# Low parts of the first feed-forward's weight tiles: by an accumulating DMA instead of VectorE

## The chip, the cores and the metric

The kernel runs on one core of a Trainium2 chip. The metric is the device time of one launch in microseconds, less being better. The engines are named as in the profile: PE (TensorE), DVE (VectorE), ACT (ScalarE), POOL (GpSimd), SP (SyncE, which here only issues DMAs).

## The reference

One inference step of a streaming encoder with two layers, on 1024 prompt frames and 64 sample frames of 1024 channels (1088 columns in all). Layer 0 mixes by windowed attention, layer 1 by a state-space model (SSM); each layer ends with a gated feed-forward with a causal convolution of width 3:

```python
def layer(x, i):
    h = rms_norm(x, g_pre)
    y = attention(h) if i == 0 else s5(h)
    x = x + rms_norm(y, g_post)
    h = rms_norm(x, g_pre_ffn)
    u = causal_conv(h @ w_up[i]) + b          # 1024 -> 2 * 2816
    y = (gelu(u[:2816]) * u[2816:]) @ w_down[i]
    return x + rms_norm(y, g_post_ffn)
```

All of it is float32, and so are the inputs and outputs. The part that matters here is `h @ w_up[0]`.

## The kernel before

**Split products.** PE multiplies in a rounded 32-bit form (fp32r). To keep float32's accuracy each operand is split into a high part, the value rounded to that form, and a low part, the rest. A product is then three matmuls in a row (`mm3`, L223 to L225): high weight by low activation, high by high, low weight by high activation.

**Weight tiles.** A weight tile is 128 x 1024 float32. `load_unit` loads it into a buffer `raw` (two of them) through SP's queue (L208 for `w_up`), and `split_unit` makes the split tile `whl` (six buffers, tag "big"):

```python
x = nc.scalar.activation(w[:, 0], raw, AF.Copy), nc.vector.tensor_sub(w[:, 1], raw, w[:, 0].bitcast(F32))
```

ACT copies raw to the high part, which rounds it; DVE subtracts that from raw and leaves the low part. Both are on L216, and both halves of `whl` are read by PE. `wsrc` lists the tiles in the order of use; `unit` hands out the next one, after `load_ahead` has asked for two more (AHEAD = 2).

**The first feed-forward.** `w_up[0]` has 44 tiles, taken as pairs 0 and 22, 1 and 23, 2 and 24, and so on: a gate tile and a value tile. For each of them PE makes the up-projection of three blocks of columns (384, 384 and 320; `up_block`, 8 x 3 matmuls each) into one of six PSUM buffers, and DVE scales it into `u` (L414). `conv` runs the convolution on ACT (L422) and DVE (L423, L424), `gate` multiplies the pair and stores it to DRAM as `gd` (L441, L442). The first three tiles (0, 22, 1) run side by side, block by block, since their blocks of activations become ready one after the other.

**The passage from attention to it.** For each block `post_norm` loads the residual `xl` (L317), multiplies by the norm (L328) and adds the residual (L331, on DVE or POOL), and the sum is stored as the new `x` (L1565). `pre_norm` then makes the activations' high part `hh` on ACT (L300) and the low part `hl` on DVE (L306) or, for three of eight slices, on POOL (L303, L304); `rstd` makes the norm (L248 to L291). While this goes on, the loads of the next weight tiles stand in SP's queue between those of `xl` and the stores of `x`.

**Beside the feed-forward.** `sums` prepares operands for the down-projection in a tile `jt`: it loads pieces of `w_down` (L355) or `gd` (L367) through SP, DVE makes four sums and differences (L358 to L361, L370 to L376), and SP stores them as `sd` or `td`. `side` prepares the SSM's tables in eight chunks: DVE and POOL multiply complex numbers (L892 to L897, tiles `m`, `tab`, `w`), PE makes `kps` (L1072) and transposes `w` into `wps` (L1083), DVE makes `kt` (L1076, L1077).

**What sets the order.** A scheduler puts each engine's instructions and each queue's DMAs into one fixed order when the kernel is built, by a simulation with priorities; each engine then runs its list in that order, and a step that waits holds back what stands behind it on the same engine or queue.

Of the kernel before, what the change touches and what calls it, by code (L numbers as in the profile page):

```python
# [8 lines left out]
F32 = mybir.dt.float32  # L9
F32R = mybir.dt.float32r  # L10
I32 = mybir.dt.int32
AF = mybir.ActivationFunctionType
ALU = mybir.AluOpType
AX = mybir.AxisListType

P = 128
D = 1024
# [5 lines left out]
KF = DFF // P  # L23
# [20 lines left out]
class Core:  # L44
# [133 lines left out]
    def load_unit(self, src):  # L178
        nc = self.nc
        raw = self.wts.tile([P, D], F32, name="raw", tag="raw", bufs=2)  # L180
        if src[0] == "w_part":

            _, i, k, s, kc, mh = src
            n = min(2, KH - k)
            if s == "s":
                ap = self.sd[:, k:k + n, kc, mh]
            else:
                k += KH * kc
                ap = self.a["w_down"][i, k:k + n, :, 512 * mh:512 * mh + 512].rearrange("k p m -> p k m")
            raw = raw[:, :512 * n]  # L190
            self.loaded = nc.sync.dma_start(raw.rearrange("p (k m) -> p k m", k=n), ap)
            w = self.big([P, 2, D], "whl")[:, :, :512 * n]
            nc.scalar.activation(w[:, 0], raw, AF.Copy)  # L193
            nc.vector.tensor_sub(w[:, 1], raw, w[:, 0].bitcast(F32))  # L194
            return w
        if src[0] == "w_sum":
            self.loaded = nc.sync.dma_start(raw.rearrange("p (h q) -> p h q", h=2), self.su[src[1], :, :, src[2]].rearrange("h p q -> p h q"))
            return self.split_unit(raw)
        ap = self.a[src[0]]
        if src[0] == "w_down":  # L200

            _, i, k, mh = src
            ap = ap[i, k:k + 2, :, 512 * mh:512 * mh + 512].rearrange("k p m -> p k m")
            self.loaded = nc.sync.dma_start(raw.rearrange("p (k m) -> p k m", k=2), ap)
        else:
            for i in src[1:]:
                ap = ap[i]
            self.loaded = nc.sync.dma_start(raw, ap)  # L208
        return self.split_unit(raw)

    behind = ()

# [1397 lines left out]
```

## Time and profile before

| | |
|---|---|
| median of three runs | 2240.71 us |
| the three runs | 2235.85, 2241.18, 2240.71 us |
| span of the profiled execution | 2241.6 us (the page gives no other time of it) |
| PE, DVE, ACT, POOL busy | 98%, 75%, 45%, 18% of the span |
| last matmuls of attention | until 366.8 us |
| passage, first part of the up-projection, part with tables beside it | 366.8 to 411, 411 to 602, 602 to 911 us |
| split line L216 on DVE, 340 to 900 us | 42 times, median 1.22 us |

A profile is one execution seen from the chip: for each instruction its line, engine, start and duration, and what released it if its engine stood idle before. A row of a group reads: line, engine, operation, output <- inputs, count. In a row of waits the left side is who waited and the right side what came last, followed by the us in all, the number of waits and the longest. In a timeline the first two numbers are start and duration in us. For a DMA the last number is the median time in us from issue to landing.

### The profile page before, as it was taken

Reading aid. Unit: us, or ns where it says so; the run is one execution under the profiler, and the core shown is the slowest. Engines: PE = TensorE matmul, PEld = TensorE weight load, DVE = VectorE, ACT = ScalarE, POOL = GpSimd, SP = SyncE. Lnnn points to the kernel's source line nnn. Section 1 sums busy time; section 2 is a strip of 40 time slices with the busy share of each in tenths; the row PEclk is TensorE's granted clock in tenths of the full one; section 3 lists DMA queues with packets and bytes.
Section 4 is the critical chain, followed back from the end, with each engine's and each line's share of the span. In section 5 each row is a group of like instructions: output and inputs, shape, how many; then the busy total and the mean of one; then the engine's idle time right before and its main releaser. Section 6 shows DMA issues by size and latency. Waiting matters only on the chain.

```text
span 2241.6 us, 36077 instructions
## 1 busy us (share of the span) xinstructions
PE 2188.9 (98%) x13875; PEld 2114.0 (94%) x13875; DVE 1687.4 (75%) x2954; ACT 1019.1 (45%) x1839; POOL 414.7 (18%) x474
## 2 busy tenths in 40 slices
PE   9999999999999999999998899999999999999997
PEld 8987789999999999999996699999999999999997
DVE  8687648989877877666768865587997788786754
ACT  5256747422333333455534742263444444455543
POOL 5322004200042323100200034352011111110000
PEclk9999999999999999999999999999999999999999
DMA  5100015656345565887749998751266667678773
GB/s 197 38 22 29 20 62 158 246 184 211 111 136 183 181 192 184 253 298 232 229 147 340 272 295 297 261 167 65 96 217 223 236 237 276 209 269 310 224 243 99
DMA packets 208124, 428.48 MB, mean 191 GB/s; under 512 B 23312, under 2 KB 114224, under 8 KB 205008
## 3 DMA queue, kind: packets, MB, share of 16 engines
q1 hardware_dynamic: 175648, 326.56, 44.3%
q0 software_dynamic: 23984, 95.12, 11.9%
q10 hardware_dynamic: 8320, 4.49, 0.9%
q8 instruction: 109, 1.79, 0.3%
q14 instruction: 63, 0.52, 0.1%
HBM read 297.75 MB, written 128.37 MB: 190 GB/s over the span
## 4 chain that ended last, share of the span: by engine, by line
PE 47%; DMA 6%; DVE 5%; ACT 1%; issue 1%; SPq 1%; POOL 0%; DVEq 0%; ACTq 0%; POOLq 0%
PE mm L225 12%; PE mm L223 12%; PE mm L224 12%; DMA raw<-in_w_down 3%; PE pb L223 1%; PE pb L225 1%; PE pa L224 1%; PE pb L224 1%; PE pa L225 1%; PE pa L223 1%; DVE whl L216 1%; ACT whl L216 1%; DMA yd<-ys 1%; DMA pm<-prm 1%; DVE y L328 0%
## 5 line engine op out<-in xcount | busy, mean ns | idle before, releaser
L223 PE MATMUL mm<-hl,whl 128*128 128x384 f32 (+1 forms) x1960 | 643.4, 329 | 3.8 <-DVE hl L306 3.1
L225 PE MATMUL mm<-hh,whl 128*128 128x384 f32 (+1 forms) x1960 | 641.1, 328 | 2.2 <-DVE whl L216 2.2
L224 PE MATMUL mm<-hh,whl 128*128 128x384 f32 (+1 forms) x1960 | 642.3, 328 | 0.0
L223 PEld LDWEIGHTS mm<-hl,whl 128*128 128x128 f32 x1960 | 368.5, 188 | 6.0 <-DVE hl L306 4.5
L225 PEld LDWEIGHTS mm<-hh,whl 128*128 128x128 f32 x1960 | 368.5, 188 | 2.9 <-DVE whl L216 2.9
L224 PEld LDWEIGHTS mm<-hh,whl 128*128 128x128 f32 x1960 | 368.7, 188 | 0.0
L216 ACT ACTIVATE whl<-raw 128x1024 fp32r<-128x1024 f32 x202 | 212.9, 1058 | 333.4 <-PE mm L225 192.2
L216 DVE TENSOR_TENSOR whl<-raw,whl 128x1024 fp32r<-128x1024 f32 x202 | 254.9, 1264 | 111.2 <-ACT whl L216 110.7
L223 PE MATMUL mm<-gt,whl 128*128 128x384 f32 (+1 forms) x968 | 316.8, 327 | 2.6 <-ACT whl L216 1.7
L225 PE MATMUL mm<-gt,whl 128*128 128x384 f32 (+1 forms) x968 | 315.8, 327 | 0.7 <-DVE whl L216 0.7
L224 PE MATMUL mm<-gt,whl 128*128 128x384 f32 (+1 forms) x968 | 315.9, 327 | 0.0
L223 PEld LDWEIGHTS mm<-gt,whl 128*128 128x128 f32 x968 | 181.7, 188 | 3.2 <-ACT whl L216 1.9
L225 PEld LDWEIGHTS mm<-gt,whl 128*128 128x128 f32 x968 | 181.6, 188 | 1.2 <-DVE whl L216 1.2
L224 PEld LDWEIGHTS mm<-gt,whl 128*128 128x128 f32 x968 | 181.7, 188 | 0.0
L194 DVE TENSOR_TENSOR whl<-raw,whl 128x1024 fp32r<-128x1024 f32 x84 | 96.3, 1153 | 69.2 <-ACT whl L193 68.2
L193 ACT ACTIVATE whl<-raw 128x1024 fp32r<-128x1024 f32 x84 | 82.6, 987 | 115.0 <-DMA raw<-sd 50.2
L423 DVE SCALAR_TENSOR_TENSOR t<-u,ppt,t 128x1090 f32<-128x1090 f32 x88 | 123.6, 1407 | 7.9 <-ACT t L422 7.3
L422 ACT ACTIVATE t<-u,ppt 128x1090 f32<-128x1090 f32 x88 | 114.2, 1298 | 24.4 <-DVE u L521 9.2
L424 DVE SCALAR_TENSOR_TENSOR t<-u,ppt,t 128x1090 f32<-128x1090 f32 x88 | 123.3, 1403 | 0.4
L414 DVE TENSOR_TENSOR u<-rb,mm 128x384 f32<-128x384 f32 (+1 forms) x164 | 80.2, 502 | 20.4 <-PE mm L225 15.7
L566 DVE TENSOR_TENSOR gt<-gr,gt 128x768 fp32r<-128x768 f32 (+2 forms) x106 | 89.9, 879 | 7.1 <-ACT gt L565 6.8
L565 ACT ACTIVATE gt<-gr 128x768 fp32r<-128x768 f32 (+2 forms) x106 | 78.4, 773 | 35.6 <-DMA gr<-gd 24.6
(390 smaller groups left out, 4113.4 us busy)
## 6 DMA issues: line engine op xcount, KB each, us to landing
raw<-in_w_up SPq DMA_DIRECT2D x88, 512.0 KB, 4.2
raw<-in_w_down SPq DMA_DIRECT2D x74, 512.0 KB, 4.4
raw<-sd SPq DMA_DIRECT2D x40, 512.0 KB, 4.6
sj<-in_w_up POOLq DMA_DIRECT2D x68, 256.0 KB, 6.1
su<-sj POOLq DMA_DIRECT2D x34, 512.0 KB, 5.8
raw<-su SPq DMA_DIRECT2D x34, 512.0 KB, 4.7
pm<-prm SPq DMA_DIRECT2D x32, 522.0 KB, 8.6
gr<-td SPq DMA_DIRECT2D x40, 384.0 KB, 5.7
```

Source lines behind the costliest of these rows:

```text
L193: nc.scalar.activation(w[:, 0], raw, AF.Copy)
L194: nc.vector.tensor_sub(w[:, 1], raw, w[:, 0].bitcast(F32))
L216: x = nc.scalar.activation(w[:, 0], raw, AF.Copy), nc.vector.tensor_sub(w[:, 1], raw, w[:, 0].bitcast(F32))
L223: nc.tensor.matmul(out, w[:, 0, sl], xl, start=start, stop=False)
L224: nc.tensor.matmul(out, w[:, 0, sl], xh, start=False, stop=False)
L225: self.last_mm = nc.tensor.matmul(out, w[:, 1, sl], xh, start=False, stop=stop)
L414: nc.vector.tensor_mul(u[:, t0 + 2:t0 + 2 + np_], rb[:, t0:t0 + np_], ps[:, :np_])
L422: nc.scalar.activation(t, u[:, 0:T + 2], AF.Identity, bias=cb(m), scale=cw(0, m))
L423: nc.vector.scalar_tensor_tensor(t, u[:, 1:T + 3], cw(1, m), t, op0=ALU.mult, op1=ALU.add)
L424: self.last_conv = nc.vector.scalar_tensor_tensor(t, u[:, 2:T + 4], cw(2, m), t, op0=ALU.mult, op1=ALU.add)
L565: nc.scalar.activation(x[:, 0, u], raw, AF.Copy)
L566: nc.vector.tensor_sub(x[:, 1, u], raw, x[:, 0, u].bitcast(F32))
```

## The change

For the tiles of `w_up[0]` other than 0, 22 and 1, that is 41 of 44, the split is made in another way. ACT copies raw to the high part as before, and copies raw a second time, with scale -1, to the low part's place, which rounds to the negated high part. A DMA from POOL's queue then adds raw onto it, which leaves raw minus the high part. DVE has no step in it. `raw` is free when that DMA has landed. All later lines move by 11 numbers.

```diff
             self.loaded = nc.sync.dma_start(raw, ap)
+        if src[0] == "w_up" and src[1] == 0 and src[2] not in (0, KF, 1):
+            return self.split_by_dma(raw)
         return self.split_unit(raw)
+
+    def split_by_dma(self, raw):
+
+        nc = self.nc
+        w = self.big([P, 2, D], "whl")
+        nc.scalar.activation(w[:, 0], raw, AF.Copy)
+        nc.scalar.activation(w[:, 1], raw, AF.Copy, scale=-1.0)
+        nc.gpsimd.dma_start(w[:, 1].bitcast(F32), raw, accum_op=ALU.add)
+        return w
```

PE's instructions are the same in number and kind, and SP's DMAs are the same; DVE has 41 steps less, ACT 41 more, POOL issues 41 DMAs more. The scheduler also lays the lists out anew. Three places follow.

SP's queue in the passage, before: the loads of weight tiles 24, 3 and 25 come after that of tile 2, all ahead of block 1's `xl`, with the store of `x` (block 0) and the first `jt` behind.

```order
L208 DMA raw_4657<-in_w_up 128x1024
L909 DMA tq_4269<-in_s_c 128x32x32
L208 DMA raw_4765<-in_w_up 128x1024
L208 DMA raw_4885<-in_w_up 128x1024
L317 DMA xl_3634<-in_x 128x2x384
L317 DMA xl_3635<-in_x 128x2x384
L317 DMA xl_3839<-in_x 128x2x320
L1565 DMA x0_90<-q_410 1024x1x384
L317 DMA xl_3840<-in_x 128x2x320
L355 DMA jt_4581<-in_w_down 128x2x1024
```

The same after (L208 is still the load; 11 is added to the other line numbers; tile 24 is raw_4659, tile 3 raw_4768, tile 25 raw_4889). Each of the three loads now waits for the accumulating DMA of the tile two before it.

```order
L208 DMA raw_4659<-in_w_up 128x1024
L208 DMA raw_4768<-in_w_up 128x1024
L328 DMA xl_3634<-in_x 128x2x384
L328 DMA xl_3635<-in_x 128x2x384
L208 DMA raw_4889<-in_w_up 128x1024
L328 DMA xl_3839<-in_x 128x2x320
L1576 DMA x0_90<-q_410 1024x1x384
L328 DMA xl_3840<-in_x 128x2x320
L366 DMA jt_4583<-in_w_down 128x2x1024
```

The load of tile 25 has moved behind two loads of `xl`; the store of `x` and the load of `jt` are behind it as before. On POOL the first two accumulating DMAs stand right behind block 0's last `hl` step, and the third behind block 1's first residual sum.

DVE in the passage, block 2: before, three of its `hl` steps stand ahead of the first `jt` sum (L358) and two steps of the norm.

```order
L331 TENSOR_TENSOR q<-q,xl 128x640
L328 TENSOR_TENSOR q<-q,pr 128x640 x2
L306 SCALAR_TENSOR_TENSOR hl<-q,ppt,hh 128x320 x3
L358 TENSOR_TENSOR jt<-jt 128x512
L271 TENSOR_SCALAR nvsqb<-pr 128x3
L272 RECIPROCAL nvsqb<-nvsqb 128x3
L359 TENSOR_TENSOR jt<-jt 128x512
```

After:

```order
L342 TENSOR_TENSOR q<-q,xl 128x640
L339 TENSOR_TENSOR q<-q,pr 128x640 x2
L369 TENSOR_TENSOR jt<-jt 128x512
L282 TENSOR_SCALAR nvsqb<-pr 128x3
L283 RECIPROCAL nvsqb<-nvsqb 128x3
L317 SCALAR_TENSOR_TENSOR hl<-q,ppt,hh 128x320 x3
L370 TENSOR_TENSOR jt<-jt 128x512
```

The `jt` sum and the two norm steps have moved ahead of the three `hl` steps.

DVE at a chunk of the tables, before: the last step of `w` (L897), which PE's `wps` reads, has an eviction (L414) and two conv steps (L423, L424) ahead of it.

```order
L894 TENSOR_TENSOR w<-m 128x4x128
L423 SCALAR_TENSOR_TENSOR t<-u,ppt,t 128x1090
L895 TENSOR_TENSOR m<-tq,tp 128x512
L896 TENSOR_TENSOR m<-tq,tp 128x512
L414 TENSOR_TENSOR u<-rb,mm 128x384
L370 TENSOR_TENSOR jt<-jt 128x384
L424 SCALAR_TENSOR_TENSOR t<-u,ppt,t 128x1090
L897 TENSOR_TENSOR w<-m 128x4x128
L374 TENSOR_TENSOR jt<-jt 128x384
L414 TENSOR_TENSOR u<-rb,mm 128x384
L375 TENSOR_TENSOR jt<-jt 128x384
L376 TENSOR_TENSOR jt<-jt 128x384
```

After, the same chunk, in which the steps of `jt` all follow `w`:

```order
L905 TENSOR_TENSOR w<-m 128x4x128
L425 TENSOR_TENSOR u<-rb,mm 128x384
L451 TENSOR_TENSOR t<-t 128x1090
L906 TENSOR_TENSOR m<-tq,tp 128x512
L907 TENSOR_TENSOR m<-tq,tp 128x512
L425 TENSOR_TENSOR u<-rb,mm 128x256
L427 TENSOR_TENSOR u<-rb,mm 128x64
L908 TENSOR_TENSOR w<-m 128x4x128
L407 MEMSET u 128x2
L434 SCALAR_TENSOR_TENSOR t<-u,ppt,t 128x1090
L425 TENSOR_TENSOR u<-rb,mm 128x384
L435 SCALAR_TENSOR_TENSOR t<-u,ppt,t 128x1090
```

The two conv steps, an eviction and the first `jt` difference now stand behind `w`; in the full list the four `jt` differences follow there, and then `kt`. On POOL, accumulating DMAs stand between the multiplications of some chunks and the last step of `tab` (L908 there).

## The prediction

> **What bounds the kernel now.** I read the page's busy shares first, then the busy time of each engine in the stretches that the change can reach, then what TensorE (PE) waits for there, and only then the groups of the changed line.
>
> The page's head, with the busy time of each engine:
>
> ```profile
> span 2241.6 us, 36077 instructions
> PE 2188.9 (98%) x13875; PEld 2114.0 (94%) x13875; DVE 1687.4 (75%) x2954; ACT 1019.1 (45%) x1839; POOL 414.7 (18%) x474
> ```
>
> PE is busy 98% of the span, so VectorE (DVE), which the change relieves, is not the bound on the average. The three stretches in which the 41 tiles are made and used come next: the passage from attention to the first feed-forward (366.8 to 411 us), its first half (411 to 602), and the half in which the tables of the next layer's SSM are prepared beside it (602 to 911).
>
> ```profile
> core 0: us, PE busy (x) PEld busy (x) DVE busy (x) ACT busy (x) POOL busy (x), PEclk, DMA share, GB/s
> 366.80:411.00 44.20, 40.71 (x255) 39.45 (x253) 42.75 (x79) 24.91 (x48) 24.74 (x16) 1.00 0.66 211
> 411.00:602.00 191.00, 190.93 (x1157) 190.63 (x1158) 172.94 (x476) 57.66 (x85) 0.93 (x2) 1.00 0.55 193
> 602.00:911.00 309.00, 301.53 (x1876) 299.31 (x1875) 229.06 (x334) 109.52 (x153) 101.94 (x72) 1.00 0.55 173
> ```
>
> PE idles 44.20 − 40.71 = 3.5 us, 0.1 us and 309.00 − 301.53 = 7.5 us. So everything that a faster supply of weights or a freer DVE could win here is 11.0 us, 0.5% of the span, at a granted clock of 1.00 throughout. The middle stretch has nothing to give, though DVE is busy 91% of it. What ended those idle times, from the view of PE's waits between 340 and 900 us (us in all, times, longest):
>
> ```profile
> PE wps L1083 <- DVE kt L1077: 5.1, 4, 1.6
> PE mm L223 <- DVE hl L306: 3.1, 3, 1.6
> PE wps L1083 <- DVE w L897: 2.4, 3, 1.1
> PE pr L266 <- DVE sqb L260: 0.4, 1, 0.4
> ```
>
> No row names the weight tile `whl`. PE waits for DVE, but for DVE's other work: the activations' low part `hl` at the passage, and the table work `kt` and `w` in the third stretch.
>
> **What the change takes away and adds.** The split line's own view, between 340 and 900 us (durations in ns: lowest, median, highest):
>
> ```profile
> L216 ACT ACTIVATE whl<-raw x42: 1037/1060/1067, 356.2 to 852.9; 128x1024 fp32r<-128x1024 f32 x42
> L216 DVE TENSOR_TENSOR whl<-raw,whl x42: 1210/1220/2409, 359.9 to 855.9; 128x1024 fp32r<-128x1024 f32 x42
> who waited for it (us, times):
>   DVE whl L216: 3.2, 7
> ```
>
> 41 of these tiles change. DVE loses 41 × 1.22 = 50.0 us. ScalarE (ACT) gains a second copy of the same shape for each, 41 × 1.06 = 43.5 us. Both are worth nothing by themselves: nobody but the subtraction itself waited for the split. ACT has the room: in the middle stretch 57.66 us plus some 18 × 1.06 = 19 is 77 of 191.
>
> GpSimd (POOL) issues 41 DMAs that the trace does not show. The nearest row for the issue itself is another DMA from POOL's queue of the same size, and the page has its time to landing, with that of the fastest DMA of 512 KB in the third stretch:
>
> ```profile
> L1400 POOL DMA_DIRECT2D su<-sj x34: 532/555/558, 1318.3 to 1446.8; - x34
> su<-sj POOLq DMA_DIRECT2D x34, 512.0 KB, 5.8
> gd<-t SPq DMA_DIRECT2D x12, 512.0 KB, 2.7
> ```
>
> Issuing costs POOL 41 × 0.555 = 22.8 us, hidden wherever POOL waits anyway (0.93 us busy of 191 in the middle stretch).
>
> The landing, D, is the unknown of this case. Below it can hardly be under 2.7 us. Above I take two plain transfers one after the other, 2 × 5.8 = 11.6, since the destination must be read as well as the source. Between them I choose 5.8 plus the time of another 512 KB at the highest rate that a slice at the passage shows:
>
> ```profile
> GB/s 0 0 9 0 0 0 139 207 73 0 163 404 400 399 216 253 189 154 286 205 126 195 102 172 153 404 288 207 295 398 188 1 0 112 395 262 419 79 245 383
> raw<-in_w_up SPq DMA_DIRECT2D x6, 512.0 KB, 5.4
> jt<-in_w_down SPq DMA_DIRECT2D x2, 1024.0 KB, 4.8
> ```
>
> 524 KB / 404 GB/s is 1.3 us, so D = 7, an estimate that leans to the row of POOL's own queue because that queue carries the new DMA. [...]
>
> **In the steady part D is hidden.** A tile is 8 × 3 × 3 = 72 matmuls, so the middle stretch passes 1157 / 72 = 16.1 tiles, 11.9 us each. Tiles are converted as buffers come free, as ACT's timeline shows:
>
> ```profile
> 459.56 1.06 ACT L216 ACTIVATE whl<-raw 128x1024 fp32r<-128x1024 f32 x1 [6.25 <-PE mm L225]
> 471.39 1.06 ACT L216 ACTIVATE whl<-raw 128x1024 fp32r<-128x1024 f32 x1 [5.56 <-PE mm L225]
> ```
>
> The split follows the end of a use by PE, 11.8 us after the one before: it is paced by PE. With six buffers of which one is in use, five others wait their turn, 5 × 11.9 = 59 us ahead. Against that stand D = 7 or 12. The other limit is the two raw buffers: load 5.4, two copies 2.1, issue 0.6 and D 7 make 15.1 us for a buffer, 7.6 a tile with two, under 11.9. That holds up to D = 2 × 11.9 − 8.1 = 15.7.
>
> **At the passage D is not hidden.** There the queues are short and every step stands behind another. Rows of POOL, ACT, SyncE's queue (SP) and DVE, each from its timeline, and one wait of SP:
>
> ```profile
> 363.63 1.07 POOL L304 TENSOR_TENSOR hl<-gx,hh 128x384 fp32r<-128x384 f32 x1
> 377.14 1.13 ACT L300 ACTIVATE hh<-q,ppt 128x384 fp32r<-128x384 f32 x2 [2.65 <-POOL q L331]
> 361.17 5.85 SPq L208 DMA_DIRECT2D raw<-in_w_up  x2
> 384.93 0.55 SPq L1565 DMA_DIRECT2D x<-q  x1
> 391.24 0.37 SPq L355 DMA_DIRECT2D jt<-in_w_down  x1
> SPq L355 <- DMA x<-q: 4.9, 1, 4.9
> 396.26 3.40 DVE L306 SCALAR_TENSOR_TENSOR hl<-q,ppt,hh 128x320 fp32r<-128x320 f32 x3
> 399.58 0.68 DVE L358 TENSOR_TENSOR jt<-jt 128x512 f32<-128x512 f32 x1
> ```
>
> By the order of the changed kernel the first two accumulating DMAs stand on POOL right behind the `hl` step that ends at 364.7. The load of tile 24 waits for the first of them to land: 364.7 + 7 = 371.7; it lands 5.4 later, at 377.1; two ACT copies end at 379.2, ahead of the `hh` copies that started at 377.14; POOL issues the third accumulation, which lands at 386.2. For that the load of tile 25 waits on SP, and behind it in SP's queue stand the store of block 0's `x` (384.93 before, now 386.9, with the issues of that load and of one `xl` ahead of it) and then the load of `jt`, which waits for that store (391.24 − 384.93 = 6.3 us): 393.2, and landed 4.8 later at 398.0. New in DVE's order is that the first `jt` addition (L358) stands ahead of block 2's three `hl` steps, where it stood behind them. So `hl`, for which PE waits, comes after 398.0 and the addition, 0.68 and some 0.2 for two tiny steps: 398.9, against 396.26 before: +2.6 us. Each us of D counts twice here. Under D of about 6.1 the store isn't held, and what stays is the 0.9 us of DVE work put ahead. At D = 11.6 it is 2.6 + 2 × 4.6 = 11.8. Block 1 is delayed on the way, its `hh` by 379.2 − 377.1 = 2.1 us; PE showed no wait for that block, and this lies on the same path, so I don't add it.
>
> **In the stretch with the tables** DVE's order changes too. The last step of `w` (L897) now stands ahead of an eviction and a conv step that it followed, so I let its three waits go: −2.4 us. `kt` still stands behind four subtractions of `jt`; its 5.1 us stay.
>
> Sum: +2.6 − 2.4 = +0.2 us, on the profiled span of 2241.6: 2241.8. That span is 0.9 us above the median of the runs, 2240.71, so I put the time at 2240.9.
>
> **Rival 1, slower: the adding DMA is slow.** The passage chain pays twice for each us of D over 6.1. About 0.3%, 6.7 us, is what a measurement of this kernel can tell from no change. That is passed from D = 9 (2.6 + 4 = 6.6) if the tables' 2.4 us don't come, and from 10.2 if they do; at 11.6 it gives 11.8 − 2.4 = +9.4, 2250. Over 15.7 the raw buffers bind as well: at D = 20 a tile takes 28.1 / 2 = 14.05 us, 2.15 more than PE needs, 88 us over 41 tiles less the 59 of lead, some 29 more. For it: the DMA reads its destination too, and the DMA share at the passage is 0.66 already. Against: 512 KB land in 2.7 to 5.8 us in all rows above.
>
> **Rival 2, slower: POOL's queue blocks.** An accumulation waits on POOL for its ACT copies, and these for PE to free a buffer. POOL runs in order, and the change puts accumulations among its table steps:
>
> ```profile
> 664.54 1.44 POOL L897 TENSOR_TENSOR tab<-m 128x576 f32<-128x576 f32 x1
> DVE m L1044 <- POOL tab L897: 6.1, 4, 2.1
> ```
>
> DVE already waits for that table in four of the chunks. A table held up for half a tile's period, 6.0 us, stops DVE, then `w` and `kt`, then PE. One such chunk stays under what can be told, two give 12 us (2253), all seven 42 (2283); it decides from two chunks on. For it: PE's waits for `w` and `kt` show no slack there. Against: POOL is busy 101.94 of 309 us, so it mostly arrives at these steps long before DVE needs them.
>
> **Rival 3, faster: DVE's relief reaches PE.** If the 50 us taken off DVE pull `hl`, `kt` and `w` forward and D is small, 3.1 + 5.1 + 2.4 = 10.6 us go: 2230. For it: all three waits are for DVE. Against: they follow chains of dependent steps and loads (`jt`) that don't shorten, and only some seven subtractions lie near any of them.
>
> **Rival 4, slower: DVE holds up POOL's DMAs.** DVE is busy 42.75 of 44.20 us at the passage, with steps of 3.40 / 3 = 1.13 us. If each accumulation waits for three such steps, D is 7 + 3.4 = 10.4, the passage costs 2.6 + 2 × 3.4 = 9.4 and the sum is +7.0: 2248. DMAs of POOL's queue beside a busy and a less busy DVE, from the DMAs of the third stretch and the busy times of the stretch in which `su` is made:
>
> ```profile
> prm<-tab POOLq DMA_DIRECT2D x14, 276.0 KB, 4.9
> 1313.00:1450.00 137.00, 137.00 (x824) 137.00 (x823) 79.38 (x170) 30.78 (x44) 62.79 (x96) 1.00 0.89 305
> ```
>
> With DVE busy 74% (229.06 of 309) 276 KB take 4.9 us; with 58% (79.38 of 137) 512 KB take 5.8, and the issue never took over 0.56. That may be a small fixed delay; it shows no hold of several us. [...]
>
> That the change doesn't do what it says is excluded: 41 subtractions are gone from DVE's order, and PE's instructions are the same in number and kind.
>
> **How the numbers follow.** Forecast (about no change): 0.64, with a range of its own of 2236 to 2247. Rival 1: 0.15, because 0.16 to 0.29 of the span between my ends of D lies above 10.2 or 9, and the row that I lean to lies below. Rival 4: 0.06, since no row shows such a hold. Rival 2: 0.09. Rival 3: 0.06. So slower by over 0.3% is 0.15 + 0.06 + 0.09 = 0.30, the same 0.64, faster 0.06. The range is 2234 to 2253: upward it takes in D at its upper end and rival 2 in two chunks, downward half of rival 3's gain and the spread of the runs before; what is left out is a D above 12, rival 2 in more chunks, and the whole of rival 3, under 2 in 10.
>
> **What would show it.** Right: the accumulating DMAs land in 6 to 8 us; PE waits at the passage for `hl` some 2 to 3 us longer, with the `x` store on SP at about 387; the middle stretch stays at 191 us for its matmuls, with no wait of PE for `whl`; `w`'s waits are gone and `kt`'s are not. Wrong: landing over 9 us, an `x` store after 390, raw loads waiting in the middle stretch with PE waiting for `whl` (rivals 1 and 4, told apart by the landing where DVE idles); POOL waiting for ACT ahead of the table steps, and PE's waits for `w` and `kt` beyond 7.5 us in all (rival 2); idle time of PE under 5 us over the three stretches (rival 3).

## The result, and the profile after

The changed kernel takes **2260.8 us** (median of four runs, 2253.8 to 2265.1) against 2240.5 for the kernel before (four runs, 2235.9 to 2241.2): a ratio of **1.0088, 95% interval 1.0070 to 1.0106**. It is 20 us slower. The forecast was 2240.9 with a range of 2234 to 2253, so the time lies above it. The profiled execution took 2265.1 us, with a span of 2263.2.

The head of its page:

```profile
span 2263.2 us, 36180 instructions
PE 2200.9 (97%) x13875; PEld 2124.6 (94%) x13875; DVE 1636.4 (72%) x2913; ACT 1057.2 (47%) x1880; POOL 439.9 (19%) x515
```

DVE lost 51 us of work, as was forecast, and PE, with the same 13875 matmuls, is busy 12 us longer. The busy times of the three stretches of the prediction, and of two short pieces of the passage, tell why:

```profile
core 0: us, PE busy (x) PEld busy (x) DVE busy (x) ACT busy (x) POOL busy (x), PEclk, DMA share, GB/s
366.80:411.00 44.20, 37.24 (x196) 36.53 (x195) 34.51 (x60) 22.51 (x45) 22.79 (x17) 0.85 0.68 191
383.00:388.00 5.00, 3.35 (x12) 3.35 (x12) 5.00 (x7) 1.56 (x3) 4.06 (x4) 0.50 0.58 184
388.00:393.00 5.00, 5.00 (x19) 5.00 (x20) 4.99 (x15) 2.96 (x5) 3.68 (x2) 0.53 0.57 214
411.00:602.00 191.00, 190.48 (x1162) 190.19 (x1161) 158.41 (x470) 73.40 (x103) 21.57 (x23) 1.00 0.81 247
602.00:911.00 309.00, 303.12 (x1881) 302.00 (x1880) 200.82 (x318) 131.24 (x178) 104.67 (x91) 0.99 0.74 209
```

In the passage PE idles 7.0 us instead of 3.5, and on top of that its clock is halved for some 10 us, in 8 of which it works: between 388 and 393 it is busy all the time and gets 19 matmuls done, where 0.18 us for each, the distance of two starts in the kernel before at 380 us, would have made 28. Before, the clock was 1.00 there. The middle stretch is as full as it was.

PE runs the same products in the same order in both kernels (in the passage a few of the 11700 records stand a place or two apart), so the start of the n-th split product in one trace minus its start in the other says at each point how much has been lost by then. The row of the changed kernel, with the columns named by the time in the kernel before (all us, worked out from the two timelines):

| | 377 | 409 | 434 | 584 | 912 | 1015 | 1059 | 1167 | 1314 | 2014 | 2067 | end |
|---|---|---|---|---|---|---|---|---|---|---|---|---|
| changed kernel | −0.3 | +7.9 | +8.7 | +8.4 | +7.5 | +9.2 | +13.3 | +13.4 | +17.0 | +17.0 | +21.2 | +21.6 |

So four places lose: the passage (8.7), the start of the down-projection (912 to 1059: 5.8), the start of the SSM (1167 to 1314: 3.6) and a place near 2052 (4.2). The steady part and the tables, for which most of the prediction's working was done, lose nothing.

**The passage, read step by step.** ACT and POOL of the changed kernel, from their timelines:

```profile
377.00 1.06 ACT L217 ACTIVATE whl<-raw 128x1024 fp32r<-128x1024 f32 x1 [3.77 <-DMA raw<-in_w_up]
379.96 1.11 ACT L311 ACTIVATE hh<-q,ppt 128x384 fp32r<-128x384 f32 x2
```

```profile
379.30 0.85 POOL L219 DMA_DIRECT2D whl<-raw  x1 [3.01 <-ACT whl L218]
379.93 1.53 POOL L314 TENSOR_SCALAR gx<-q,ppt 128x384 f32<-128x384 f32 x1
381.15 2.07 POOL L342 TENSOR_TENSOR q<-q,xl 128x768 f32<-128x768 f32 x1
382.96 1.21 POOL L315 TENSOR_TENSOR hl<-gx,hh 128x384 fp32r<-128x384 f32 x1
```

ACT's copies of tile 24 wait 3.77 us for a load that itself waited for the first accumulating DMA, and block 1's `hh` stands behind them in ACT's list: 379.96 instead of 377.14. What that does to DVE and PE:

```profile
380.60 4.00 DVE L317 SCALAR_TENSOR_TENSOR hl<-q,ppt,hh 128x384 fp32r<-128x384 f32 x1 [0.72 <-ACT hh L311]
404.10 0.68 DVE L369 TENSOR_TENSOR jt<-jt 128x512 f32<-128x512 f32 x1
404.85 3.50 DVE L317 SCALAR_TENSOR_TENSOR hl<-q,ppt,hh 128x320 fp32r<-128x320 f32 x3
```

```profile
380.07 0.34 PE L236 MATMUL mm<-hh,whl 128*128 128x384 f32 x1
384.65 0.69 PE L234 MATMUL mm<-hl,whl 128*128 128x384 f32 x1 [4.24 <-DVE hl L317]
```

Block 1's first `hl` starts late, lies beside three POOL steps in a row, and takes 4.00 us; PE, which has finished block 0 at 380.4, waits 4.24 us for it. In that wait, at 382.5, the granted clock falls to a half. The same `hl` in the kernel before, and PE's last matmul of block 0 there:

```profile
378.63 0.61 DVE L306 SCALAR_TENSOR_TENSOR hl<-q,ppt,hh 128x384 fp32r<-128x384 f32 x1
380.37 0.33 PE L225 MATMUL mm<-hh,whl 128*128 128x384 f32 x1
```

It was done at 379.24, and PE ended block 0 at 380.7: the slack was some 1.5 us, which a delay of 2 us uses up.

### The profile page after: what moved, and what is told of

The parts are those of the page before. It is cut to its first block, busy times and chain, and to the rows that moved or that the text cites. A ratio compares the mean times of both kernels' runs of the same rounds, so it can differ in the third digit from the quotient of the medians.

```text
span 2263.2 us, 36180 instructions
## 1 busy us (share of the span) xinstructions
PE 2200.9 (97%) x13875; PEld 2124.6 (94%) x13875; DVE 1636.4 (72%) x2913; ACT 1057.2 (47%) x1880; POOL 439.9 (19%) x515
## 4 chain that ended last, share of the span: by engine, by line
PE 35%; DMA 13%; DVE 8%; ACT 3%; issue 2%; SPq 1%; POOL 0%; ACTq 0%; DVEq 0%; POOLq 0%
PE mm L234 8%; PE mm L236 8%; PE mm L235 8%; DMA raw<-in_w_down 4%; DMA raw<-sd 3%; DMA gr<-gd 2%; DVE whl L194 2%; PE pb L234 1%; PE pb L236 1%; PE pa L235 1%; PE pb L235 1%; PE pa L236 1%; PE pa L234 1%; ACT whl L193 1%; DMA yd<-ys 1%
## 5 line engine op out<-in xcount | busy, mean ns | idle before, releaser
L227 DVE TENSOR_TENSOR whl<-raw,whl 128x1024 fp32r<-128x1024 f32 x161 | 199.0, 1239 | 106.8 <-ACT whl L227 106.4
L227 ACT ACTIVATE whl<-raw 128x1024 fp32r<-128x1024 f32 x161 | 169.7, 1058 | 225.5 <-PE mm L236 82.9
L194 DVE TENSOR_TENSOR whl<-raw,whl 128x1024 fp32r<-128x1024 f32 x84 | 96.2, 1154 | 80.8 <-ACT whl L193 80.1
L193 ACT ACTIVATE whl<-raw 128x1024 fp32r<-128x1024 f32 x84 | 82.5, 986 | 109.5 <-DMA raw<-sd 51.0
L433 ACT ACTIVATE t<-u,ppt 128x1090 f32<-128x1090 f32 x88 | 114.2, 1298 | 36.3 <-DVE u L532 12.9
L342 POOL TENSOR_TENSOR y<-y,xl 128x768 f32<-128x768 f32 (+1 forms) x16 | 32.4, 2024 | 339.7 <-DVE y L339 271.3
```

The source lines that it names most:

```text
L342: x = by[q].tensor_add(yq, yq, xs[q])
L433: nc.scalar.activation(t, u[:, 0:T + 2], AF.Identity, bias=cb(m), scale=cw(0, m))
```

## The experiments

**Theory.** The loss comes from a few places where PE had a slack of about a us, each of which the change uses up in its own way, and a gap of PE of some 2 us or more costs about twice its length, since the clock is halved in it or behind it (in the passage above, 0.50 between 383 and 388 us and 0.53 between 388 and 393). **Rivals**: the adding itself loads the DMA engines (A); POOL's queue or the copies on ACT cost it everywhere (B); the loss is in the lists that the scheduler laid anew, not in the operations (C). All kernels share the products, so the places of the table above serve for all of them; here are its columns 409, 434, 584, 912, 1059, 1314 and the end, each from one profiled execution:

| kernel | 409 | 434 | 584 | 912 | 1059 | 1314 | end |
|---|---|---|---|---|---|---|---|
| changed kernel | +7.9 | +8.7 | +8.4 | +7.5 | +13.3 | +17.0 | +21.6 |
| the same again | +8.6 | +8.6 | +8.3 | +8.1 | +11.3 | +14.7 | +13.7 |
| late_start | +0.9 | +5.1 | +4.8 | +5.2 | +11.1 | +10.6 | +13.9 |
| passage_only | +6.1 | +6.1 | +6.1 | +3.6 | +3.6 | +1.5 | +1.5 |
| copies_later | +2.6 | +2.9 | +8.3 | +7.5 | +15.0 | +15.4 | +20.5 |
| filled_gap | +11.7 | +11.3 | +11.0 | +11.1 | +16.0 | +18.7 | +17.6 |
| plain_copy | +3.2 | +5.0 | +4.6 | −2.7 | +0.8 | +1.3 | +6.0 |
| tl_first | +7.9 | +7.9 | +7.6 | +10.5 | +10.5 | +12.8 | +11.7 |
| middle_only | +1.2 | +1.2 | +2.3 | +6.6 | +6.6 | +8.6 | +14.4 |
| tail_only | −0.7 | −0.7 | −0.7 | +15.7 | +16.5 | +14.9 | +16.0 |
| repaired | +1.7 | +1.7 | +1.4 | +1.1 | +2.3 | +0.4 | +3.4 |
| copies_alone | +4.6 | +4.7 | +9.6 | +23.0 | +26.9 | +32.9 | +31.9 |

**late_start.** The three tiles made in the passage keep the subtraction.

```diff
-        if src[0] == "w_up" and src[1] == 0 and src[2] not in (0, KF, 1):
+        if src[0] == "w_up" and src[1] == 0 and src[2] not in (0, KF, 1, KF + 1, 2, KF + 2):
```

> The split by DMA only from tile 3 on: tiles 23, 2 and 24, which are made in the passage, are split as before (38 tiles changed). Theory A: the loss comes from the passage, where ACT waits for tile 24's raw load ahead of block 1's activations and PE then stands for 4.2 us and gets half its clock for 10 us. Then the passage costs nothing here and the time is 2240 to 2245 us, with no half clock between 370 and 420 us. Rival B: the extra traffic of the 41 adding DMAs (DMA share 0.81 against 0.55) delays loads all along. Then 38 of 41 tiles keep nearly all of the loss: 2256 to 2262. Rival C: half of the loss lies in later stages and has nothing to do with the passage: 2250 to 2253.

2257.28 against 2240.6, ratio 1.0071 (1.0047 to 1.0096): not the 2240 to 2245 that was expected if the passage is all, but a time within the 2256 to 2262 of the rival, extra traffic. The passage is clean (+0.9), so what was lost there hangs on those three tiles; but a new place right behind it takes 4.2 us. Its waits of PE between 415 and 440, and DVE's timeline there:

```profile
PE mm L234 <- DVE u L427: 2.4, 1, 2.4
```

```profile
423.60 0.17 DVE L1031 TENSOR_TENSOR dv<-dv,ppt 128x8 f32<-128x8 f32 x1 [3.60 <-DMA dv<-in_s_d]
```

DVE waits for a load of 4 KB of the SSM's parameters, and the eviction that PE needs stands behind that. The load took 10.0 us from issue to landing, in the kernel before 6.0; the first two accumulating DMAs run beside it. They need not be the cause: the same load took 3.8 us beside two of them when the changed kernel was run again, and 8.9 beside two plain copies (plain_copy, below).

**passage_only.** The other way round: only those three tiles by the accumulating DMA.

```diff
-        if src[0] == "w_up" and src[1] == 0 and src[2] not in (0, KF, 1):
+        if src[0] == "w_up" and src[1] == 0 and src[2] in (KF + 1, 2, KF + 2):
```

> The opposite part: only tiles 23, 2 and 24 are split by DMA, 38 as before. Theory A: the whole passage loss stays, +8 us and more with a gap of PE over 3 us near 380 us and half clock behind it: 2249 to 2260. Rival B (traffic): 3 of 41 DMAs, no loss that can be told, 2239 to 2243. Rival C: the passage part alone, about 2249.

2251.84 (ten runs, 2244.9 to 2257.7) against 2240.6, ratio 1.0045 (1.0027 to 1.0062). The profiled run is the fastest of the ten (2244.9), so its later columns are not typical. It has +6.1 in the passage, with the second half of the predicted path in it (DVE waits 1.75 us for the load of `jt` in front of block 2's `hl`, PE 4.34 us behind that). For block 1 PE waits only 0.74 us for `hl` and 1.61 for a step of the norm, not the 3 us and more that were expected. Three accumulating DMAs cost more than half of what 41 cost.

**copies_later.** ACT's copies of tile 24 are put behind block 1's last `hh`; all 41 DMAs stay. The scheduler laid the lists anew for it: the load of tile 25 went behind that of `jt` on SP, and the first `jt` sum behind two of block 2's `hl` steps on DVE.

```diff
+        x = nc.scalar.activation(w[:, 0], raw, AF.Copy), nc.scalar.activation(w[:, 1], raw, AF.Copy, scale=-1.0)
+        if behind is not None:
+            self.order(x[0], behind)
+            self.order(x[1], behind)
```

> The changed kernel with one order more: ACT's two copies of tile 24 must come behind block 1's last hh. All 41 DMAs stay. Theory A: block 1's hh and hl are on time, no gap of PE over 2 us near 380 us, granted clock 1.0 there: 8 us less than the changed kernel, 2252 or less. Rival B (traffic): 2258 to 2263, as the changed kernel.

2261.03 against 2240.6, ratio 1.0084 (1.0057 to 1.0110). The passage falls from +8.7 to +2.9. Block 1's gap is gone, as it should be if the copies in front of `hh` caused it; block 2's order changed as well, so not all of the 5.8 us are theirs. The time doesn't follow (2252 or less was expected). Between 434 and 584 a gap that the changed kernel hasn't takes 5.4 us, at an eviction that stands in DVE's list behind two conv steps and a row of small SSM steps. Ahead of those DVE waited 1.42 us for `dv`, which now took 13.3 us to land. The waits of PE between 425 and 450:

```profile
PE mm L236 <- DVE u L429: 3.9, 1, 3.9
```

**filled_gap.** Six matmuls on idle data, 128 x 512, are pinned between block 0 and block 1, to keep PE busy in its gap.

```diff
+                if i == 0 and b == 1 and len(ms) == 3 and ms[0] == 0:
+                    self.pin = self.fill(self.mm_ps("idle"), 6, 512, self.last_mm)
```

> The changed kernel with six matmuls of 128x512 whose result nobody reads, in PE's order between block 0's products and block 1's, so that PE works while it waits for block 1's hl. Theory A, with the half clock a consequence of the gap: the wait stays (hl is no earlier), the half clock of 10 us behind it goes, 5 us less than the changed kernel: 2254 to 2257. If the half clock has another cause (load, power), or fills cost as much as they save: 2258 to 2264.

2263.54 against 2240.6, ratio 1.0102 (1.0073 to 1.0131); 2254 to 2257 was expected. The clock between 380 and 402 is 1.00, and the passage still loses 11.7. The six matmuls, 12 records on PE, took 5.31 us; and in this run block 1's first `hl` was not stretched (0.62 us, done at 382.34; the step behind it took 3.40), so the fill outlasted the wait for that step:

```profile
381.34 5.31 PE L246 MATMUL idle<-ppt,ident 128*128 128x512 f32 x12
```

The lists were laid anew, with a `jt` sum in front of block 2's multiply on DVE, and a gap of 4.12 us stands at block 2:

```profile
401.44 0.69 DVE L374 TENSOR_TENSOR jt<-jt 128x512 f32<-128x512 f32 x1 [4.52 <-DMA jt<-in_w_down]
```

A busy PE keeping its clock fits the theory, but the run gave no gain to show by it what the halved clock is worth.

**plain_copy.** The same 41 DMAs without the addition, which leaves raw in the low part's place, so that the products are not the reference's; every list is that of the changed kernel. This separates the adding (A) from the lists (C).

```diff
-        nc.gpsimd.dma_start(w[:, 1].bitcast(F32), raw, accum_op=ALU.add)
+        nc.gpsimd.dma_start(w[:, 1].bitcast(F32), raw)
```

> The changed kernel with the same 41 DMAs as plain copies: they overwrite the low part with raw and don't add (so the low part is not the low part, and the products are not the reference's). Every engine's order is that of the changed kernel. Theory: the adding itself makes these DMAs slow and crowds the others out. Then they land in 4 to 5 us instead of 6.0, the 4 KB load of dv beside them in 6 us or less instead of 8.9, and the time falls by 3 to 8 us, to 2253 to 2258. Rival: only the order of the lists and the wait for a landing cost, whatever the DMA does: 2258 to 2263.

2249.95 (ten runs, 2243.2 to 2258.8) against 2241.1, ratio 1.0038 (1.0023 to 1.0053), below the 2253 to 2258 of the theory. The ten runs of the changed kernel in this study have a mean of 2258.3, these ten 2249.6: the adding itself costs 8.7 us (95% interval 4.6 to 12.9), about half of the loss. The order, the copies and the transfer as such cost the other half. The transfers by queue and by kind between 430 and 602 us, of the changed kernel and of this one (`software_dynamic` is POOL's queue; the last number of its row is its share of the 16 DMA engines' time):

```profile
q0 software_dynamic: 2173, 7.88, 24.6%
...
raw<-in_w_up SPq DMA_DIRECT2D x17, 512.0 KB, 6.0
whl<-raw POOLq DMA_DIRECT2D x15, 512.0 KB, 6.3
...
gd<-t SPq DMA_DIRECT2D x8, 32.0 KB, 7.0
```

```profile
q0 software_dynamic: 2304, 8.39, 12.2%
...
whl<-raw POOLq DMA_DIRECT2D x16, 512.0 KB, 4.0
raw<-in_w_up SPq DMA_DIRECT2D x16, 512.0 KB, 4.4
gd<-t SPq DMA_DIRECT2D x8, 32.0 KB, 4.0
```

For each byte the adding DMA holds the engines twice as long (24.6 / 7.88 = 3.1% per MB, 12.2 / 8.39 = 1.45), and the others pay: a load of `raw` takes 6.0 us against 4.4 (4.7 in the second profile of the changed kernel, so this one varies), a small store 7.0 against 4.0 (6.6 in the second profile). The kernel before has 4.1 and 3.1 there:

```profile
raw<-in_w_up SPq DMA_DIRECT2D x14, 512.0 KB, 4.1
...
gd<-t SPq DMA_DIRECT2D x8, 32.0 KB, 3.1
```

The passage shows how it costs time: with plain copies the first of these DMAs lands in 4.8 us instead of 6.4, ACT waits 1.96 us for tile 24 where it waited 3.77, and the half clock at 383 to 388 is gone, while block 2 still waits 5.0 us for its `hl` behind `jt`. One part of the expectation failed: the load of `dv` took 8.92 us here too, not 6 or less.

**tl_first.** In the changed kernel two large loads for the down-projection (`gr`, L588) stand in SP's list ahead of the last loads of `tl`, the SSM's small operand tiles; here they are held behind them.

```diff
-                    nc.sync.dma_start(r[:, :n], gd[:, 6 * x:6 * x + n, :384])
+                    y = nc.sync.dma_start(r[:, :n], gd[:, 6 * x:6 * x + n, :384])
+                    if i == 0:
+                        self.order(y, self.last_tl)
```

> The changed kernel, with the two large gr loads for the down-projection held behind the last chunk's tl loads in SP's list, as in the kernel before; nothing else in any engine's order moves. Theory: that place in the list is why the first down-projection starts with its loads 3 us behind and PE stands 2 us near 1036 us with half clock behind it. Then that gap goes and the stage's 4.1 us come back: 2255 to 2258. Rival: the gap comes from traffic or chance and stays: 2259 to 2263.

2254.77 against 2241.1, ratio 1.0061 (1.0043 to 1.0080), 3 to 6 us less than the two medians of the changed kernel (the means differ by 3.8 us, with an interval of −0.6 to 8.2, so the times alone don't settle it). The loss at the down-projection (912 to 1059) is gone, from +5.8 to 0.0. That loss, in the changed kernel, is a chain of late weight loads; its ACT row, its DVE row and its wait of PE:

```profile
1034.06 1.06 ACT L193 ACTIVATE whl<-raw 128x1024 fp32r<-128x1024 f32 x1 [3.23 <-DMA raw<-in_w_down]
```

```profile
1035.15 1.23 DVE L194 TENSOR_TENSOR whl<-raw,whl 128x1024 fp32r<-128x1024 f32 x1 [3.07 <-ACT whl L193]
```

```profile
PE mm L234 <- DVE y L627: 2.1, 1, 2.1
```

The `y` eviction stands behind that DVE step. With the order mended `tl` lands in 2.3 us instead of 7.8, and this wait is absent. The other kernels agree: the six profiles with `gr` ahead of `tl` lose 3.2 to 7.5 us between 912 and 1059, and of the six changed ones without it five lose 1.2 at most (copies_alone 3.9). These lists lie beyond 911 us, past the last accumulating DMA: they moved because the scheduler laid them anew.

**middle_only and tail_only.** The accumulating DMA only for the tiles 5 to 16 of each half, or only for 17 to 21.

```diff
+        if src[0] == "w_up" and src[1] == 0 and 5 <= src[2] % KF <= 16:
...
+        if src[0] == "w_up" and src[1] == 0 and src[2] % KF >= 17:
```

> The split by DMA for pairs 5 to 16 alone (24 tiles), which are made after the passage and its small loads and used before or at the start of the tables. Theory: in the steady part the DMA is hidden, so nothing is lost: 2238 to 2244, no gap of PE over 1.8 us between 370 and 1150 us. Rival (traffic of the adding DMAs costs all along): over half of the loss, 2252 or more.

> The split by DMA for pairs 17 to 21 alone (10 tiles), made while the tables are prepared. SP's list at the last chunk is that of the kernel before. Theory: no passage loss and no loss in the down-projection; in the tables the waits for w and kt change by a us or two either way: 2238 to 2245. Rival (the tables' loads are crowded out by the adding DMAs): PE waits for kt above 7 us and gaps over 2 us there, 2247 or more.

middle_only: 2255.0 against 2241.1, ratio 1.0065 (1.0050 to 1.0080), where 2238 to 2244 was expected. The steady part costs 1.1 us, so the prediction that it is hidden held; the tables take 4.3 and what lies behind them 7.8. tail_only: 2258.68, ratio 1.0083 (1.0066 to 1.0101), where 2238 to 2245 was expected, and 16.4 us of it in the tables. Its largest row of PE's waits between 340 and 940, and the DVE row with the longest wait there:

```profile
PE wps L1094 <- DVE w L908: 13.7, 4, 7.8
```

```profile
770.52 0.56 DVE L381 TENSOR_TENSOR jt<-jt 128x384 f32<-128x384 f32 x1 [5.66 <-DMA jt<-gd]
```

DVE's new list has `w` behind a `jt` difference whose load is late; PE waits 7.8 us, and its clock is halved for 10.2 us, from 2.3 us into the wait. The load wasn't crowded out: it took 4.6 us, in the kernel before 6.8, but went out at 765.92 instead of 762.40, and DVE's list has the difference ahead of the first step of `w`, where the kernel before has it behind. The same ten DMAs are part of the full change, which loses nothing in that stretch. That speaks for rival C.

**repaired.** All but the first tiles by DMA (the passage and what comes right behind it keep the subtraction), with the order of tl_first.

```diff
-        if src[0] == "w_up" and src[1] == 0 and src[2] not in (0, KF, 1):
+        if src[0] == "w_up" and src[1] == 0 and src[2] % KF >= 4:
```

> The split by DMA from pair 4 on (36 tiles), so that no adding DMA lies in the passage or beside the small loads behind it, and the two gr loads held behind the tables' last tl loads. In the SSM the second yf load stands behind the U loads again, as before. Theory (a hold in the passage, small loads crowded out behind it, and lists laid out anew in the down-projection and the SSM make the loss): passage, down-projection and SSM cost nothing, the steady part 1 us at most, the tables 0 to 4: 2240 to 2247. Rival (36 adding DMAs still crowd out the chain of loads in the tables, whatever the order): 2250 or more, with PE's waits for kt and w above 10 us.

2247.05 (ten runs, 2243.6 to 2258.8) against 2240.55, ratio 1.0037 (1.0020 to 1.0053). Its waits of PE between 340 and 940 are almost those of the kernel before:

```profile
PE wps L1096 <- DVE kt L1090: 5.9, 6, 2.0
PE mm L234 <- DVE hl L317: 3.1, 3, 1.6
```

36 accumulating DMAs then cost 6.5 us, where 41 cost 20, and where middle_only with 24 and tail_only with 10 of these 36 cost 14 and 18. So the loss doesn't go by the number of these DMAs but by single places, which move with the lists; and yet there is no gain: DVE's relief reaches PE nowhere.

**copies_alone.** No DMA at all: ACT makes both copies, DVE adds raw onto the second one.

```diff
-        nc.gpsimd.dma_start(w[:, 1].bitcast(F32), raw, accum_op=ALU.add)
+        nc.vector.tensor_add(w[:, 1], raw, w[:, 1].bitcast(F32))
```

> ACT makes both copies as in the changed kernel, but DVE adds raw onto the negated one instead of the DMA (41 tiles): ACT's 43 us more without the DMAs. Theory: ACT's copies are off the path and raw comes free as early as before, so nothing holds the passage: 2238 to 2245, no gap of PE over 2 us between 370 and 450 us. Rival (ACT's second copy itself is what delays block 1's activations): a gap over 3 us near 380 us and 2248 or more.

2277.5 against 2240.55, ratio 1.0156 (1.0133 to 1.0180): the slowest of all, and my expectation fell. Its waits of PE between 340 and 940:

```profile
PE wps L1094 <- DVE kt L1088: 15.0, 6, 3.5
PE mm L234 <- DVE u L425: 3.5, 1, 3.5
```

Compared with the kernel before, ACT is busy 39.5 us longer (1058.6 against 1019.1) and DVE's step waits for two copies instead of one; the lists are new as well. Which of these it is stays open. What it shows is that ACT's second copy and new lists can lose more than the whole change does, without one accumulating DMA.

**again.** The changed kernel unaltered, to see which of the four places come back.

> The changed kernel once more, unaltered, for a second profile of it. What its lists and waits cause comes back: a gap of PE near 380 us with half clock (8 us by the first products after the passage), a gap near 1036 us (4 us), a wait for pm of about 4 us in the SSM near 1260 us (3 us). What was chance does not: the gap near 2052 us, which none of the other kernels with the same lists showed. Then the span is 2253 to 2260; if the later gap is as fixed as the others, 2260 to 2265.

2257.63 (six runs, 2250.5 to 2262.8) against 2240.29, ratio 1.0075 (1.0057 to 1.0094). Its waits of PE between 340 and 1150:

```profile
PE mm L234 <- DVE hl L317: 8.3, 2, 4.2
PE wps L1094 <- DVE kt L1088: 6.4, 4, 2.7
PE mm L234 <- DVE y L627: 1.4, 2, 0.9
```

The passage comes back (+8.6), the down-projection with part of its loss (+3.2 from 912 to 1059), the SSM too (+3.4 from 1059 to 1314). The gap near 2052 doesn't: it belongs to one execution, and the 4.2 us of it are no part of the cause.

## Why the prediction was wrong

**The step that failed** is this one: "Block 1 is delayed on the way, its `hh` by 379.2 − 377.1 = 2.1 us; PE showed no wait for that block, and this lies on the same path, so I don't add it." The delay was about right (379.96 against 377.14, 2.8 us). Both reasons for leaving it out were wrong. That PE showed no wait for block 1 said only that its slack wasn't negative; the rows of the kernel before have it at 1.5 us, less than the delay. And it has a path of its own to PE, which waits for block 1's `hl` some 20 us before it comes to block 2. late_start and copies_later, in which this delay is absent, have no such wait, and by 409 they have lost 0.9 and 2.6 us instead of 7.9 (both have other lists too).

**What a late step costs.** The prediction let a wait cost its own length. Here a delay of 2.8 us met a DVE step stretched by 3.4, which made a gap of 4.24 us on PE; and the half clock, 8 us of it behind the gap, took about 4 more.

**The predicted path to block 2** began as forecast: the load of tile 24 issued at 370.85 (371.7 forecast), the copies done at 379.0 (379.2). Then it failed. The third accumulation landed 4.8 us after its issue, not 7, the load of tile 25 went out at 384.10, and SP was free for the store of `x` at about 384.9, where it stood before. The store left at 389.10, because it waited for DVE:

```profile
384.10 0.34 SPq L208 DMA_DIRECT2D raw<-in_w_up  x1
389.10 0.56 SPq L1576 DMA_DIRECT2D x<-q  x1
SPq L1576 <- DVE hl L317: 4.7, 1, 4.7
388.12 0.94 DVE L342 TENSOR_TENSOR q<-q,xl 128x768 f32<-128x768 f32 x1
399.58 1.55 DVE L339 TENSOR_TENSOR q<-q,pr 128x640 f32<-128x640 f32 x2 [3.27 <-PE pr L295]
```

This store is block 1's, not block 0's as the prediction and the section on the change have it (block 0's left at 358.20), and it left right after block 1's last residual sum, which ended at 389.06, behind the stretched `hl`. So the delay of block 1 made it late, and not the load of tile 25. The load of `jt` followed at 395.35 and landed at 400.6, but DVE didn't wait for it: it had stood 3.27 us for PE's norm products, and came to the `jt` sum at 404.10. PE waits 2.7 us for block 2 where it waited 3.1 before, so the +2.6 of the sum isn't there. By the prediction's own rule, with the landings that were measured (6.4 and 4.8 us), the store isn't held and 0.9 us are left. In passage_only and plain_copy DVE does wait for `jt` (1.75 and 1.77 us), but there too the store had waited for DVE.

**D** was taken as 7, and its median is 6.0. The view of the changed line, between 340 and 900 us:

```profile
L219 POOL DMA_DIRECT2D whl<-raw x41: 846/857/918, 364.4 to 866.0; - x41
...
  ACT whl L218: 174.8, 21
...
DMA to landing us min/median/max: 4.5/6.0/9.6
```

Its issue costs POOL 0.857 us, not 0.555, which is hidden; and the 0.56 that rival 4 has for the issue holds for `su` alone, since the issues of `prm` (L1094) took 0.75 to 0.82 us in the kernel before. Rival 1, which needed a D of 9 or more in the passage, is thereby out: the three accumulations there land in 6.4, 6.0 and 4.8 us. But the adding does cost, in a way that no rival had: it takes twice the engines' time (3.1% per MB against 1.45 in plain_copy), and some *other* transfers land later beside it (the 32 KB store after 7.0 and 6.6 us against 4.0). All in all the adding costs 8.7 ± 4.1 us (plain_copy).

**The tables.** The waits for `w` went, as forecast, and `kt` kept its own (5.9 us against 5.1). PE's three largest rows between 340 and 940:

```profile
PE mm L234 <- DVE hl L317: 7.0, 2, 4.2
PE wps L1094 <- DVE kt L1088: 5.9, 4, 2.6
PE mm L234 <- DVE gt L577: 1.5, 1, 1.5
```

POOL did wait for ACT, 174.8 us in 21 waits, but PE's waits for `kt` and `w` come to 5.9 us, under the 7.5 that rival 2 needed: it is out for the changed kernel. Rival 3 (relief) brought nothing, by repaired too. Rival 4 can't be it: it needed every landing at 10.4 us, and half of the 41 land within 6.0.

**Beyond 911 us** the prediction looked at nothing. The scheduler moved `gr` ahead of `tl` there, which cost up to 5.8 us (tl_first takes it away). In the SSM it put the second `yf` load ahead of the third `U` loads (`yf`, `U` and `pm` are tiles that the SSM loads). All eight profiles with that order have a wait of PE for `pm` of 3.5 to 4.5 us, the other five 1.0 to 2.0. That is a correlation, and passage_only has the order and the wait (3.9 us) and loses nothing between 1167 and 1314; no kernel changed that order alone, so it stays open whether it is the cause.

**How the 20 us divide.** In the two profiles of the changed kernel: 8.7 and 8.6 by the end of the passage, 5.8 and 3.2 at the start of the down-projection, 3.7 and 3.4 from there to 1314; the rest changes from execution to execution (+21.6 and +13.7 at the end). Seen the other way, 8.7 ± 4.1 us come from the adding; what is left, about 9, lies in the new lists, the copies on ACT and the transfers as such, which no run parts cleanly. No version was faster than the kernel before.

## What to carry to other kernels

Where PE shows no wait, work out its slack from the two rows on either side, and set it against every delay that the change makes there; a gap on PE can cost more than its length (here the one of 2.4 us near 2052 cost 4.2, with the clock at 0.5 for 3.4 us behind it). An operation taken off a busy engine gives nothing unless a wait of the bounding engine ends at it (DVE lost 51 us of work here, and the kernel took 20 us longer), and the transfer that replaces it can make others late (here it held 24.6% of the DMA engines' time between 430 and 602 us, and a 32 KB store landed there after 7.0 us instead of 3.1). With a scheduler that lays out all lists anew, look through the whole program's order for moved loads, not only where the edit stands, and count such moves as a cost of some us even for an edit that touches ten tiles.

## What the hardware showed that I had not expected

**The clock at a gap.** Over the thirteen profiles, between 360 and 1150 and between 1320 and 2200 us, PE has 38 gaps of 1.85 us or more; with 35 of them the granted clock goes to 0.5, in the gap or up to 2.1 us behind it, for 3.4 us (27 times), 6.8 (6) or 10.2 (2). The other three gaps are 2.6 to 2.9 us long. Of 32 gaps between 1.0 and 1.85 us, 3 have it, and so have two of 0.95 us near 397 (late_start, middle_only). The kernel before has no gap over 1.59 there. In the changed kernel the gap of 4.24 us at 380.4 has the clock at 0.5 for 10.2 us, from 382.5 on, and the one of 2.4 us, which ends at 2054.97, for 3.4 us from 2055.0 on. Why some gaps have it for 3.4 us and others for two or three times as long, no run shows.

**DVE beside POOL.** The `hl` step of 0.61 us took 4.00 us while POOL ran three steps back to back (rows above): it ended 0.4 us after the third of them. It took 4.00 us in again and tl_first too; in passage_only and filled_gap it came through in 0.62, and the next DVE step took 3.4 instead. No run moved POOL's steps alone, so it isn't shown that they are the cause.

**Small transfers beside large ones** are hit, but unevenly. The 32 KB store went from 3.1 us to 4.0 beside plain copies and 7.0 beside adding ones. The 4 KB `dv` load, 6.0 us before, took 8.9, 10.0 and 13.3 beside two adding DMAs in three kernels, but 3.8, 5.1 and 3.9 in three others (again, tl_first, filled_gap), and 8.9 beside two plain copies; so no run shows that the adding is what delays it.
